# Two running sums for the expert outputs, conditional weight loads, and two weight splits per block on GpSimd, in a decoder layer with 64 experts

## The chip, the cores and the metric

The kernel runs on one core of a Trainium2 chip. The metric is the device time of one execution in microseconds (us), and the smaller the better. The engines are named as in the profile: PE (TensorE, matmul; PEld is its loading of weights), DVE (VectorE), ACT (ScalarE), POOL or Pool (GpSimd), SP (SyncE, which here only issues transfers). Lines such as L1171 are lines of the kernel before, unless the text says that they are of the changed kernel.

## What is computed

One decoder layer on 512 tokens of width 1024, in float32. Three token mixers are projected, gated and summed, and a residual is added. Behind it stands the part that the change touches: a mixture of 64 experts of width 256, eight for each token, and one shared expert, then a residual and a last norm.

```python
def moe_ffn(h, router_w, router_bias, w1, w3, w2, sw1, sw3, sw2):
    scores = sigmoid(xt @ router_w)                 # 512 x 64
    ...                                             # the best 8 of 64 experts for each token, weights W
    for each expert e, for its tokens t:
        out[t] += W[t, e] * ((silu(xt[t] @ w1[e]) * (xt[t] @ w3[e])) @ w2[e])
    out += (silu(xt @ sw1) * (xt @ sw3)) @ sw2      # shared expert
x = x + gate * out
return rmsnorm(x, final_norm)
```

(The loop over experts is written here as what it amounts to.) Which tokens an expert gets is known only on the chip, so the kernel makes lists of work and runs loops whose lengths it reads from them.

## The kernel before

The program is one long order of work. On these inputs it goes through these stages (times of the profiled execution): input projection and the three mixers to 838 us; the gated sum of the projected branches, 838 to 928 us; output projection and routing, 931 to 1060; shared expert and **pairs** of expert runs, 1060 to 1500; **blocks** of what is left, 1508 to 1617; last norm, 1617 to 1644.

Matmuls are done to more than the precision of one pass: each operand is split in a high half (rounded, by ACT, L49) and a low half (the rest, a subtraction, L50), and three matmuls are summed (high by high, low by high, high by low). `split(hi, lo, src)` puts the low half on DVE unless it is told another engine.

An expert's slots fall into runs. A long run (up to 256 slots, "a") and a short one (up to 64, "c") are computed together in `pair_of_runs`; what is left goes by blocks of 128 slots in `block(i)`. There are 16 pairs and 9 blocks here. Both loops are nests of `tc.If(n > i)`, so every engine compares and branches once per turn (L1311, L1316).

One block on the engines:
- PE: the up projection of this block (24 matmuls of 128x512, L1133 to L1135, `ph`), transposes of the next block's tokens (`pt`, L1126), transposes of the activated product (`p`, L1151), the down projection (12 matmuls, `py`, L1163 to L1165).
- ACT and DVE: the splits of the *next* block's weights, six pieces of 128x1024 per block. `wh[u]` on ACT, then `wl[u]` on DVE, for u = 0 to 3 (up, from the raw tile `ra`) and u = 4, 5 (down, from `rad`). Between them stand, in order, the activation `hw` (ACT, then DVE L1143), the splits of the tokens (`mT_hi`, `mT_lo`) and of the activated product (`hh`, `hl`), and `y` (DVE L1167). On DVE the order is wl0, wl1, wl2, hw, wl3, sa, mT_lo, hl, mT_lo, y, y, wl4, wl5.
- Pool: copies the next list row (`ia`, L1102), gathers the tokens (`xg`, L1104), and at the end issues an indirect transfer that adds `y` into the sum `acc` in DRAM (L1171). Each add waits for the one before it on the same sum, since they may hit the same rows.
- SP: loads the raw weights for the block after the next (L990, L996; 3.1 MB per block), into the buffers that the splits have read. It does so also past the end of the list, where the row of the list names some expert anyway.

`acc` is 768 x 1024 floats: 512 tokens and 256 rows for empty slots. It begins as the residual stream, its last 256 rows zeroed by four ACT-queue transfers beside the gated sum (L758). Short runs add to it by halves of rows, through the view `accc` (L1218). At the end four token tiles are loaded from it (`fm`, L1333, issued by SP), squared (ACT L1334), scaled (Pool L1336 and L70, DVE L1338) and stored (L1339).

Of the kernel before, what the change touches and what calls it, by code (L numbers as in the profile page):

```python
# [34 lines left out]
def trunk(ctx, tc, x, c, ada_w, ada_b, norm1, norm2, w_in, conv_a_w, conv_a_b, ln_a_g, ln_a_b,  # L35
# [21 lines left out]
    # ---------------------------------------------------------------- constants  # L57
# [20 lines left out]
    acc = dram.tile([S + 2 * P, D], F32, name="acc")  # L78
# [14 lines left out]
    # ---------------------------------------------------------------- parameters in columns  # L93
# [6 lines left out]
    for name, ap, n in plist:  # L100
        if at % P + n > P or name == "mu":  # the first two are wanted before the others
            at = (at // P + 1) * P
        off[name] = at
        at += n
# [10 lines left out]
    # ---------------------------------------------------------------- input projection  # L115
# [68 lines left out]
    # shift and scale of two channel tiles at a time; the first columns' weights come in between  # L184
# [18 lines left out]
    # RMSNorm statistics and the transposed normalised stream  # L203
# [19 lines left out]
    abv = cols("ab", 16).rearrange("p (z k) -> p z k", z=2)  # of shift and 1 + scale  # L223
# [36 lines left out]
    # ---------------------------------------------------------------- RWKV  # L260
# [17 lines left out]
    zd = dram.tile([16, P, S], F32, name="zd")  # mixed conv 0-3, RWKV 4-7, LRU 8-15  # L278
    gd = dram.tile([24, P, S], F32, name="gd")  # branch gates, tanh of half
# [7 lines left out]
    # masks over (head, s) rows and t columns  # L287
# [4 lines left out]
    mask = rp.tile([P, 2, CH], F32, name="mask")  # s < t, s <= t  # L292
    V.tensor_scalar(mask[:, 0], tcol, srow, None, op0=OP.is_gt)
    V.tensor_scalar(mask[:, 1], tcol, srow, None, op0=OP.is_ge)
    lev = rp.tile([P, 6, CH], BF, name="lev")  # block-doubling masks
# [12 lines left out]
    bones = rp.tile([P, P], F32, name="bones")  # head block of ones  # L308
# [7 lines left out]
    smask = rp.tile([P, S], BF, name="smask")  # 0 where a chunk starts  # L316
# [8 lines left out]
    hcol = rp.tile([P, 12], F32, name="hcol")  # halves of w0, a0, k_a  # L325
# [27 lines left out]
    # ---------------------------------------------------------------- rest of the modulation, as rows  # L353
    def modulation(g4):
# [9 lines left out]
        if g4 // 2 == 2:  # norm2 (1 + scale)  # L364
# [5 lines left out]
    UC = 4           # chunks per unit  # L370
    US = UC * CH     # tokens per unit
    HQ = (slice(0, CH), slice(CH, P))  # rows of either head
    identc = rp.tile([P, CH], F32, name="identc")  # an identity per head
# [6 lines left out]
    def over(t, n=UC):  # the same for each chunk  # L380
        return t[:, None].to_broadcast([t.shape[0], n, *t.shape[1:]])
# [4 lines left out]
    # products per chunk and head: each head has its rows of the array, and its bank  # L386
    class Heads:
# [16 lines left out]
        def turn(s, src):  # L404
            for i in range(UC):
                for h, q in enumerate(HQ):
                    if h:  # a transpose proper leaves its result from row 0 on
# [9 lines left out]
    # a power of a sum over each head's channels, on all of them: token-major for the power, and back  # L417
# [14 lines left out]
    def unit(c, hf):  # L432
# [6 lines left out]
        # sigmoid(x) = (1 + tanh(x / 2)) / 2  # L439
# [5 lines left out]
        # decay: exp(w) = exp(-1/2) sigmoid(w0 + ...), summed within each chunk  # L445
# [7 lines left out]
        # the removal key's norm, squared, goes with the one of its two factors that is summed over  # L453
# [12 lines left out]
        # time-major: rows (head, token). zt: Z, Azk V, V; bt: A_zb^T, A_qb^T, B, K; at: A_zk^T, A_qk^T  # L466
# [16 lines left out]
        # bonus  # L483
# [6 lines left out]
        # T = (I + A)^-1 of 32-token blocks and its transpose, by block doubling  # L490
        inv = rp.tile([P, 2, UC, CH], F32, name="inv", bufs=2)  # T^T, T
# [19 lines left out]
        # [W | U0] = (I + A)^-1 [Z | Azk V], here negated  # L511
# [742 lines left out]
    def block(i):  # L1254
        if i:
            load_up(ra, GL, i + 2)
# [3 lines left out]
        for u in range(4):  # L1260
            up_a(ph, u)
            if u < 3:
                split_a(i + 1, u, up)
# [106 lines left out]
```

## Time and profile before

| | |
|---|---|
| runs, us | 1646.1, 1631.59, 1632.52; median 1632.52 |
| profiled execution: span | 1644.2 us; the run nearest to it is 1646.1 |
| PE busy | 1460.9 us, 89% |
| PEld, DVE | 1045.2 (64%), 1032.0 (63%) |
| ACT, POOL | 611.6 (37%), 580.6 (35%) |

A row of the timeline is start, duration, engine, line, operation, output<-input, then in brackets how long the engine had been idle and what ended that. A row of a table by stretches gives for each engine the busy us in the stretch and the number of instructions, then the TensorE clock that was granted (1.00 is 2.4 GHz, 0.50 is 1.2 GHz), the share of the DMA engines' time and GB/s. Busy shares are means over stages with different limits, so each edit is to be read in the stage where it stands.

### The profile page before, as it was taken

What the parts mean: (1) busy time and instruction counts of PE and PEld (TensorE: products, weight loads), DVE (VectorE), ACT (ScalarE), POOL (GpSimd) and SP (SyncE); (2) the same over time, 40 slices, a digit from 0 to 9 for tenths busy, and PEclk for the clock granted to TensorE, in tenths of its full rate; (3) what the DMA queues carried; (4) which work ended last, traced back from release to release, by engine and by line L of the source; (5) the groups of instructions that cost most, each with busy time, mean ns of one, the idle gap of its engine ahead of it and who ended that gap; (6) DMA issues with size and microseconds to landing.
All of it is one profiled execution on the core that took longest, in us unless ns stands there. A gap on an engine that the chain in (4) does not pass through costs nothing. (4 is left out here: it accounts for less than half of the span.)

```text
span 1644.2 us, 23961 instructions
## 1 busy us (share of the span) xinstructions
PE 1460.9 (89%) x8794; PEld 1045.2 (64%) x8794; DVE 1032.0 (63%) x1803; ACT 611.6 (37%) x981; POOL 580.6 (35%) x457
## 2 busy tenths in 40 slices
PE   4998897989999989999699986797999999997883
PEld 3765565656666666566478764565777777775662
DVE  7747879796843246656825476664656656565884
ACT  4432132222442326336422242152443444433763
POOL 3222433132222223234765266433333334232322
PEclk7989888898999979989899999898999999998997
DMA  9324434021222112113475353499999999996996
GB/s 336 110 76 123 151 90 145 26 81 39 68 85 75 39 30 62 46 39 100 125 245 200 145 169 129 126 321 341 326 330 327 330 324 336 333 327 158 339 312 208
DMA packets 202140, 294.85 MB, mean 179 GB/s; under 512 B 13484, under 2 KB 155062, under 8 KB 202002
## 3 DMA queue, kind: packets, MB, share of 16 engines
q1 hardware_dynamic: 181490, 244.97, 44.3%
q0 software_dynamic: 17904, 44.90, 11.8%
q10 hardware_dynamic: 2608, 3.24, 0.6%
q8 instruction: 74, 1.21, 0.3%
q14 instruction: 64, 0.52, 0.1%
HBM read 258.15 MB, written 45.92 MB: 185 GB/s over the span
## 5 line engine op out<-in xcount | busy, mean ns | idle before, releaser
L50 POOL TENSOR_TENSOR w_lo<-w_raw,w_hi 128x1024 fp32r<-128x1024 f32 x76 | 195.1, 2571 | 335.2 <-ACT w_hi L49 333.2
L53 PE MATMUL ps_in<-hT_hi,w_hi 128*128 128x512 f32 x496 | 216.1, 436 | 5.8 <-ACT hT_hi L49 3.3
L54 PE MATMUL ps_in<-hT_hi,w_lo 128*128 128x512 f32 x496 | 214.2, 432 | 7.2 <-POOL w_lo L50 7.2
L55 PE MATMUL ps_in<-hT_lo,w_hi 128*128 128x512 f32 x496 | 211.6, 430 | 0.0
L50 DVE TENSOR_TENSOR wl<-ra,wh 128x1024 fp32r<-128x1024 f32 x100 | 121.6, 1224 | 105.7 <-ACT wh L49 103.5
L1133 PE MATMUL ph<-wh,mT_hi 128*128 128x512 f32 x360 | 144.9, 403 | 14.0 <-issue 10.1
L49 ACT ACTIVATE wh<-ra 128x1024 fp32r<-128x1024 f32 x100 | 105.9, 1062 | 105.9 <-PE ph L1135 102.4
L1134 PE MATMUL ph<-wl,mT_hi 128*128 128x512 f32 x360 | 143.5, 399 | 0.5 <-DVE wl L50 0.5
L1135 PE MATMUL ph<-wh,mT_lo 128*128 128x512 f32 x360 | 142.8, 397 | 0.0
L1171 POOL DMA_INDIRECT acc<-y,sa x41 | 72.2, 1761 | 155.8 <-DVE hc L1207 121.0
L53 PEld LDWEIGHTS ps_in<-hT_hi,w_hi 128*128 128x128 f32 x496 | 98.1, 198 | 37.7 <-issue 9.6
L54 PEld LDWEIGHTS ps_in<-hT_hi,w_lo 128*128 128x128 f32 x496 | 97.9, 197 | 32.1 <-POOL w_lo L50 8.1
L55 PEld LDWEIGHTS ps_in<-hT_lo,w_hi 128*128 128x128 f32 x496 | 98.2, 198 | 24.5 <-issue 5.0
L597 DVE SCALAR_TENSOR_TENSOR u<-ut,par,u 128x512 f32<-128x512 f32 x120 | 100.1, 857 | 1.2
L49 ACT ACTIVATE w_hi<-w_raw 128x1024 fp32r<-128x1024 f32 x76 | 79.6, 1053 | 56.2 <-PE ps_p L55 27.0
L498 POOL TENSOR_TENSOR Bm<-bt,lev 128x256 f32<-128x256 f32 x40 | 28.8, 736 | 168.3 <-DVE bt L480 101.9
L49 ACT ACTIVATE wh<-rad 128x1024 fp32r<-128x1024 f32 x52 | 52.4, 1055 | 95.4 <-PE py L1165 39.0
L1133 PEld LDWEIGHTS ph<-wh,mT_hi 128*128 128x128 f32 x360 | 69.3, 192 | 29.3 <-issue 11.0
L1167 DVE TENSOR_TENSOR y<-py,rows 128x512 f32<-128x512 f32 x82 | 56.5, 690 | 44.5 <-PE py L1165 43.8
L1134 PEld LDWEIGHTS ph<-wl,mT_hi 128*128 128x128 f32 x360 | 69.3, 193 | 15.2 <-DVE wl L50 1.0
L1135 PEld LDWEIGHTS ph<-wh,mT_lo 128*128 128x128 f32 x360 | 69.2, 192 | 14.5
L1163 PE MATMUL py<-wh,hh 128*128 128x512 f32 x180 | 76.4, 424 | 1.5 <-ACT hh L49 0.7
(524 smaller groups left out, 3105.8 us busy)
## 6 DMA issues: line engine op xcount, KB each, us to landing
ra<-in_exp_w_dram SPq DMA_DIRECT2D x52, 1024.0 KB
rc<-in_exp_w_dram SPq DMA_DIRECT2D x34, 1024.0 KB
w_raw<-in_w_in_dram SPq DMA_DIRECT2D x31, 1024.0 KB
rad<-in_exp_w_dram SPq DMA_DIRECT2D x27, 1024.0 KB
ada<-in_ada_w_dram SPq DMA_DIRECT2D x64, 256.0 KB
rcd<-in_exp_w_dram SPq DMA_DIRECT2D x16, 1024.0 KB
ada<-in_ada_w_dram SPq DMA_DIRECT2D x8, 1024.0 KB
gd<-sg SPq DMA_DIRECT2D x24, 256.0 KB
```

What stands on the lines that cost most here:

```text
L49: A.activation(hi, src, AF.Copy)
L50: (lo_engine or V).tensor_tensor(lo, src, hi.bitcast(F32), op=OP.subtract)
L53: T.matmul(ps, l[0], r[0], start=first, stop=False)
L54: T.matmul(ps, l[1], r[0], start=False, stop=False)
L55: T.matmul(ps, l[0], r[1], start=False, stop=last)
L597: V.scalar_tensor_tensor(u[:, ct], ut[ct][:, w:w + S], col("caw", w * 4 + ct), u[:, ct], op0=OP.mult, op1=OP.add)
L1133: T.matmul(ph[b], h2T[0][b][:, k], wh[u][:, q], start=(k == 0), stop=False)
L1134: T.matmul(ph[b], h2T[0][b][:, k], wl[u][:, q], start=False, stop=False)
L1135: T.matmul(ph[b], h2T[1][b][:, k], wh[u][:, q], start=False, stop=(k == KT - 1))
L1163: T.matmul(py, hT[0][:, k], wh[4 + k][:, q], start=(k == 0), stop=False)
L1167: V.tensor_tensor(y[:, q], py, gate[:, q], op=OP.mult)
L1171: st = G.indirect_dma_start(out=acc, out_offset=IOA(ap=at, axis=0), in_=y, in_offset=None, compute_op=OP.add, bounds_check=S + 2 * P - 1, ...
```

## The change

There are four edits.

1. A second sum `acc2` of the same size. It is zeroed whole by two ACT-queue transfers behind the four that zero the last rows of `acc`. Short runs (through `accc`) add to it; long runs still add to `acc`; blocks add to the two in turn.
2. In `block` the weight loads stand in a `tc.If(n_left > i + 2)`.
3. In `block` the low halves of pieces 0 and 2 are computed by Pool; pieces 1, 3, 4 and 5 stay on DVE.
4. At the end each token tile is loaded from both sums (SP and ACT queue) and DVE adds the two, before the square.

```diff
-    acc = dram.tile([S + 2 * P, D], F32, name="acc")
+    acc, acc2 = (dram.tile([S + 2 * P, D], F32, name=n) for n in ("acc", "acc2"))
...
         nc.scalar.dma_start(acc[S + h // 2 * P:...], z0...)
+    a2v = acc2.rearrange("(g p) d -> p g d", p=P)
+    for h in range(2):
+        nc.scalar.dma_start(a2v[:, :, h * 512:h * 512 + 512],
+                            z0.rearrange("p c x -> p (c x)")[:, None].to_broadcast([P, (S + 2 * P) // P, 512]))
...
-    h2c, accc = (t.rearrange("t (a d) -> (t a) d", a=2) for t in (h2d, acc))
+    h2c, accc = (t.rearrange("t (a d) -> (t a) d", a=2) for t in (h2d, acc2))
...
-    def split_a(j, u, up=None):
-        split(wh[u], wl[u], ...)
+    def split_a(j, u, up=None, lo_engine=None):
+        split(wh[u], wl[u], ..., lo_engine)
...
-    def add_a(y, at, beside=None):
-        st = G.indirect_dma_start(out=acc, ...
+    def add_a(y, at, beside=None, to=acc):
+        st = G.indirect_dma_start(out=to, ...
...
     def block(i):
-        if i:
-            load_up(ra, GL, i + 2)
         up = rc[0] if i == 1 else None
-        load_down(rad[i % 2], GL, i + 2)
+        with tc.If(n_left > i + 2):
+            if i:
+                load_up(ra, GL, i + 2)
+            load_down(rad[i % 2], GL, i + 2)
...
             if u < 3:
-                split_a(i + 1, u, up)
+                split_a(i + 1, u, up, V if u == 1 else G)
...
-        add_a(down_a(hT, gm2), sa[:, 0, 0:1])
+        add_a(down_a(hT, gm2), sa[:, 0, 0:1], to=(acc, acc2)[i % 2])
...
         nc.sync.dma_start(m, acc[t * P:(t + 1) * P])
+        m2 = fp.tile([P, D], F32, name="fm2", bufs=4)
+        nc.scalar.dma_start(m2, acc2[t * P:(t + 1) * P])
+        V.tensor_tensor(m, m, m2, op=OP.add)
         A.activation(sq, m, AF.Square, scale=1.0 / 32, accum_out=fs[:, t:t + 1])
```

How it moves instructions is seen in the order of each engine's program. First Pool, one block, before (L1316 is the loop's branch; `ra`, `wh`, `wl` are raw weights, high and low halves):

```order
L1316 COMPARE_AND_BRANCH
L1101 TENSOR_LOAD items
L1101 ISA x2
L1102 ISA
L1102 COPY ia_8120<-idxw 128x4
L1104 DMA xg_8102<-h2d,ia_8120 128x1024
L1171 DMA acc<-y,sa 768x1024
```

The same block on Pool in the changed kernel (its lines are some numbers higher; wl_7159 and wl_7161 are pieces 0 and 2):

```order
L1323 COMPARE_AND_BRANCH
L1262 COMPARE_AND_BRANCH
L1262 UNCONDITIONAL_BRANCH x2
L50 TENSOR_TENSOR wl_7159<-ra_7921,wh_7153 128x1024
L50 TENSOR_TENSOR wl_7161<-ra_7921,wh_7155 128x1024
L1106 TENSOR_LOAD items
L1106 ISA x2
L1107 ISA
L1107 COPY ia_8123<-idxw 128x4
L1109 DMA xg_8105<-h2d,ia_8123 128x1024
L1177 DMA acc<-y,sa 768x1024
```

Two subtractions and the inner branch now stand ahead of the gather, right behind the add of the block before. On DVE the same block before, up to the low half of the activated product (wl_7156 to wl_7159 are pieces 0 to 3):

```order
L1316 COMPARE_AND_BRANCH
L50 TENSOR_TENSOR wl_7156<-ra_7918,wh_7150 128x1024
L50 TENSOR_TENSOR wl_7157<-ra_7918,wh_7151 128x1024
L50 TENSOR_TENSOR wl_7158<-ra_7918,wh_7152 128x1024
L1143 SCALAR_TENSOR_TENSOR hw<-hw,ia_8120,ph 128x256
L50 TENSOR_TENSOR wl_7159<-ra_7918,wh_7153 128x1024
L1117 COPY sa<-ia_8120 128x4
L50 TENSOR_TENSOR mT_lo_6263<-pt,mT_hi_6261 128x512
L50 TENSOR_TENSOR hl<-p_16619,hh 128x256
```

And on DVE in the changed kernel (wl_7160 and wl_7162 are pieces 1 and 3):

```order
L1323 COMPARE_AND_BRANCH
L1262 COMPARE_AND_BRANCH
L1262 UNCONDITIONAL_BRANCH x2
L50 TENSOR_TENSOR wl_7160<-ra_7921,wh_7154 128x1024
L1149 SCALAR_TENSOR_TENSOR hw<-hw,ia_8123,ph 128x256
L50 TENSOR_TENSOR wl_7162<-ra_7921,wh_7156 128x1024
L1122 COPY sa<-ia_8123 128x4
L50 TENSOR_TENSOR mT_lo_6264<-pt,mT_hi_6262 128x512
L50 TENSOR_TENSOR hl<-p_16625,hh 128x256
```

DVE keeps piece 1 ahead of `hw` and piece 3 behind it; the two pieces that stood around piece 1 are gone. Last, ACT in the tail, before (behind the loop's branches; `fnb` is the last norm's weight row, `fsq` the square):

```order
L1316 UNCONDITIONAL_BRANCH x97
L1329 ACTIVATE fnb<-fnp 128x512
L1334 ACTIVATE fsq,fs<-fm 128x1024
L1329 ACTIVATE fnb<-fnp 128x512
L1334 ACTIVATE fsq,fs<-fm 128x1024 x3
```

And in the changed kernel, where the rows of L1342 are the loads from `acc2` (printed as acc_73) into the four `fm2` tiles:

```order
L1323 UNCONDITIONAL_BRANCH x97
L1342 DMA fm_27765<-acc_73 128x1024
L1342 DMA fm_27776<-acc_73 128x1024
L1336 ACTIVATE fnb<-fnp 128x512
L1342 DMA fm_27787<-acc_73 128x1024
L1336 ACTIVATE fnb<-fnp 128x512
L1344 ACTIVATE fsq,fs<-fm 128x1024 x2
L1342 DMA fm_27798<-acc_73 128x1024
L1344 ACTIVATE fsq,fs<-fm 128x1024 x2
```

The fourth load from `acc2` now stands behind two squares on ACT, which wait for DVE's adds.

## Rows read from the trace of the kernel before

**Rows 1.** The page's head: span of the profiled execution.

```profile
span 1644.2 us, 23961 instructions
```

**Rows 2.** Stretches: busy us per engine, PE clock, DMA share, GB/s.

```profile
core 0: us, PE busy (x) PEld busy (x) DVE busy (x) ACT busy (x) POOL busy (x), PEclk, DMA share, GB/s
852.00:856.00 4.00, 4.00 (x19) 3.23 (x18) 1.72 (x4) 0.83 (x1) 0.00 (x0) 1.00 1.08 384
...
1433.00:1459.00 26.00, 26.00 (x142) 18.96 (x144) 15.66 (x24) 10.99 (x17) 9.45 (x10) 1.00 1.06 333
...
1558.00:1571.00 13.00, 11.36 (x47) 8.60 (x46) 10.04 (x14) 7.96 (x10) 3.30 (x4) 0.87 1.05 332
...
1616.00:1620.00 4.00, 0.55 (x3) 0.11 (x1) 2.96 (x3) 1.94 (x2) 2.32 (x1) 1.00 0.06 14
1628.00:1632.00 4.00, 1.31 (x2) 0.00 (x0) 0.02 (x1) 2.26 (x4) 0.81 (x2) 0.50 0.98 374
```

**Rows 3.** Timeline of one block: start, duration, engine, line, operation, idle before it.

```profile
1544.55 0.39 PE L1133 MATMUL ph<-wh,mT_hi 128*128 128x512 f32 x1
1545.72 2.32 POOL L1171 DMA_INDIRECT acc<-y,sa  x1 [2.49 <-DVE y L1167]
1547.52 1.07 ACT L49 ACTIVATE wh<-ra 128x1024 fp32r<-128x1024 f32 x1 [0.29 <-PE ph L1135]
1547.63 3.58 DVE L50 TENSOR_TENSOR wl<-ra,wh 128x1024 fp32r<-128x1024 f32 x3
...
1550.48 1.05 ACT L49 ACTIVATE wh<-ra 128x1024 fp32r<-128x1024 f32 x1
1551.12 0.47 DVE L1143 SCALAR_TENSOR_TENSOR hw<-hw,ia,ph 128x256 f32<-128x256 f32 x1
...
1551.56 1.23 DVE L50 TENSOR_TENSOR wl<-ra,wh 128x1024 fp32r<-128x1024 f32 x1
...
1553.37 0.41 DVE L50 TENSOR_TENSOR hl<-p,hh 128x256 fp32r<-128x256 f32 x1
...
1553.84 0.51 PE L1165 MATMUL py<-wh,hl 128*128 128x512 f32 x1 [0.49 <-DVE hl L50]
...
1556.25 0.39 PE L1133 MATMUL ph<-wh,mT_hi 128*128 128x512 f32 x1
```

**Rows 4.** Groups by line, 1507 to 1618: count, busy us, mean ns, idle before.

```profile
L1171 POOL DMA_INDIRECT acc<-y,sa x9 | 20.9, 2319 | 24.4 <-DVE y L1167 24.4
```

**Rows 5.** Timeline, output projection: the same subtraction on DVE and Pool.

```profile
932.89 5.78 POOL L50 TENSOR_TENSOR wo_lo<-wr,wo_hi 128x1024 fp32r<-128x1024 f32 x2 [1.14 <-ACT wo_hi L49]
933.78 2.64 DVE L50 TENSOR_TENSOR wo_lo<-wr,wo_hi 128x1024 fp32r<-128x1024 f32 x1 [0.67 <-ACT wo_hi L49]
```

**Rows 6.** Line L50, two of its groups: ns of one, min/median/max.

```profile
L50 DVE TENSOR_TENSOR wo_lo<-wr,wo_hi x4: 1224/1675/2642, 931.9 to 946.9; 128x1024 fp32r<-128x1024 f32 x4
L50 POOL TENSOR_TENSOR wo_lo<-wr,wo_hi x4: 2452/2929/3369, 932.9 to 948.0; 128x1024 fp32r<-128x1024 f32 x4
```

**Rows 7.** Timeline, gated sum, behind the zeroing: weights landing, split, used.

```profile
855.17 2.01 ACT L49 ACTIVATE w_hi<-w_raw 128x1024 fp32r<-128x1024 f32 x2 [3.42 <-DMA w_raw<-in_proj_b_dram]
856.31 4.91 POOL L50 TENSOR_TENSOR w_lo<-w_raw,w_hi 128x1024 fp32r<-128x1024 f32 x2 [8.59 <-ACT w_hi L49]
...
860.82 0.40 PE L54 MATMUL ps_p<-z_hi,w_lo 128*128 128x512 f32 x1
```

**Rows 8.** Timeline of the tail: first and last square, last scaling.

```profile
1629.74 1.06 ACT L1334 ACTIVATE fsq<-fm 128x1024 f32<-128x1024 f32 x1 [2.56 <-DMA fm<-acc]
...
1634.06 1.06 ACT L1334 ACTIVATE fsq<-fm 128x1024 f32<-128x1024 f32 x1
...
1638.13 1.28 DVE L1338 SCALAR_TENSOR_TENSOR fm<-fm,fs,fnb 128x1024 f32<-128x1024 f32 x1 [0.77 <-POOL fs L70]
```

**Rows 9.** Line L1316, PE's branches at the turns of the block loop, ns.

```profile
L1316 PEldq COMPARE_BRANCH  x11: 65/65/3336, 1507.4 to 1617.6; - x11
```

**Rows 10.** Timeline, pairs: the Pool adds that wait for the add before.

```profile
1122.20 1.59 POOL L1171 DMA_INDIRECT acc<-y,sa  x1 [5.65 <-DMA acc<-yc,sc__8497]
...
1482.43 2.06 POOL L1218 DMA_INDIRECT acc<-yc,sc__12172  x1 [7.72 <-DMA acc<-y,sa]
...
1505.96 1.59 POOL L1218 DMA_INDIRECT acc<-yc,sc__12434  x1 [5.60 <-DMA acc<-y,sa]
```

More of the change, by code (lines that the diff above doesn't have):

```diff
@@ L1118, in slots @@
         return t
-    def split_a(j, u, up=None):
-        split(wh[u], wl[u], (up or ra[j % 2])[:, u * 1024:(u + 1) * 1024] if u < 4 else rad[j % 2][:, (u - 4) * 1024:(u - 3) * 1024])
+    def split_a(j, u, up=None, lo_engine=None):
+        split(wh[u], wl[u], (up or ra[j % 2])[:, u * 1024:(u + 1) * 1024] if u < 4 else rad[j % 2][:, (u - 4) * 1024:(u - 3) * 1024],
+              lo_engine)
     def x_a(b, g):
@@ L1168, in down_a @@
         return y
-    def add_a(y, at, beside=None):
-        st = G.indirect_dma_start(out=acc, out_offset=IOA(ap=at, axis=0), in_=y, in_offset=None,
+    def add_a(y, at, beside=None, to=acc):
+        st = G.indirect_dma_start(out=to, out_offset=IOA(ap=at, axis=0), in_=y, in_offset=None,
                                   compute_op=OP.add, bounds_check=S + 2 * P - 1, oob_is_err=True)
```

## The prediction

> **What bounds the kernel now.** I read the page's head first, then the table by stretches, because the change touches four stages with different limits. The span is 1644.2 us [rows 1]; the run nearest to it is 1646.1, so 1.9 us lie around the span and the profiled execution's own time is 1646.1, 0.8% above the median of 1632.52. In the pairs PE is busy 26.00 us of 26 [rows 2]: PE bounds them, and only what makes PE wait there can cost or gain anything. In the gated sum PE is also full while the DMA engines are full too (4.00 of 4, share 1.08, 384 GB/s at 852 to 856) [rows 2], so a transfer added there stands in line with those that PE needs. In the tail PE has nothing to do; the transfers (374 GB/s) [rows 2], the squares and the scalings are the path.
>
> In a block PE is the bound, but not alone. The timeline of one block shows it: PE starts at 1544.55 and the next block at 1556.25, 11.70 us later, and before the down projection's first use of `hl` PE had to wait for DVE (1553.84, idle 0.49, ended by `hl`) [rows 3]. Behind that stands a chain on DVE: wl0 to wl2 end at 1551.21, `hw` at 1551.59, wl3 at 1552.79, then `sa`, `mT_lo` and `hl`, which ends at 1553.78 [rows 3]. wl3 begins when ACT's wh3 is done (1551.53) [rows 3]. So whatever delays wl3 delays `hl` and with it PE, one for one; nothing lies between to take it up.
>
> **The sum of two parts, by turns (edit 1).** In the blocks each add should wait for the add before it. The groups by line show that it never did: all nine adds of the block stage had their idle time, 24.4 us in all, ended by DVE's `y`, none by an add [rows 4]. Gain there: 0. In the pairs three adds did wait for another sum's landing: 5.65, 7.72 and 5.60 us, 19.0 in all [rows 10]. These waits vanish, but Pool is not what ends the stage: PE is full through the pairs [rows 2]. I take 0; if that cover did not hold, up to 19.0 would be gained (a rival below). The waits' removal also lets Pool leave the pairs earlier, so the halves that it now makes for the first block start without delay; that is why I add nothing for that one.
>
> **Zeroing `acc2`.** 768 x 1024 x 4 bytes are 3.15 MB. At the 384 GB/s of a full stretch [rows 2] that is 8.2 us of all DMA engines, in a stage where they are full. What is late next is the raw weights of the gated sum: they landed at 855.17, Pool's first low half from them began at 856.31 and two of them took 4.91, so the first was ready near 858.8, and PE used one first at 860.82 at the latest [rows 7]. Slack 2.0. If the zeros go ahead of those weights whole, PE stalls 8.2 - 2.0 = 6.2; if the weights' queue keeps its turn, nothing. I take the middle, **3** (0 to 6).
>
> **Weight loads behind a condition (edit 2).** Two blocks of nine no longer load, 2 x 3.1 MB. The DMA engines were at a share of 0.06 at 1616 to 1620 and nothing in the block's path waits for them [rows 2, 3]; gain 0. The inner condition costs each engine a compare and a jump per block. PE's compare takes 65 ns in the median [rows 9]; 9 x 2 x 65 ns is 1.2 at most, run ahead by the sequencer while matmuls drain. I take 0 (0 to 1.2).
>
> **Two low halves on Pool (edit 3).** DVE loses two subtractions of 1.2 us per block. What that could gain: `hw` began at 1551.12 though ACT's part of it was done when ACT began wh3 at 1550.48, so up to 0.6 on `hw`; but wl3 still waits for wh3, which ended 0.03 before wl3 began [rows 3], so the path to `hl` gains about nothing. What it could cost: Pool takes 2.45 for what DVE does in 1.22 [rows 6], and the two do not run side by side. Where both did this same subtraction, DVE's began at 933.78, during Pool's (932.89 to 935.34), and ended at 936.42: 1.08 behind Pool's end, 2.64 instead of 1.22; the Pool operation behind it took 3.3 (5.78 for the two; 3.37 at most) [rows 5, 6]. I lay that pattern into the block, in us from the block's start:
>
> - Pool is free when its add is issued: it begins at 1.17 and takes 2.32 [rows 3], or 1.59 as adds do in the pairs [rows 10]: free at 2.76 to 3.49. wl0 ends at 5.2 to 5.9.
> - DVE's wl1 is ready at 4.04 (wh1 ends at 1548.59) [rows 3], in the middle of wl0: held, it ends at 6.3 to 7.0. `hw` ends at 6.8 to 7.5; before, 7.04.
> - Pool's wl2 begins at 5.2 to 5.9, shares time with wl1, takes 3.37: ends at 8.6 to 9.3.
> - DVE's wl3 is ready at 7.0 to 7.5: held by wl2, it ends 1.08 after it, at 9.65 to 10.4; before, 8.24 [rows 3].
>
> So `hl`, the down projection and the next block come 1.4 to 2.15 later in each of nine blocks [rows 4]: 12.7 to 19.4, I take **16**. The `hw`, `mT_lo` and `hl` operations read PSUM; I count no hold for them. The Trainium skill, page "SBUF — State Buffer", section "Who interferes with whom", speaks against this edit: a DVE instruction with two SBUF inputs contends with a GpSimd instruction that reads SBUF, and the second to issue fully blocks. The trace agrees that DVE is held to beyond the end of Pool's operation; by the rule the held one would end a whole 1.22 after it rather than 1.08, which would make this term 1.3 larger.
>
> **The clock.** PE's idle time before the down projection grows from about 0.5 to between 1.9 and 2.6 per block. One block before the change already lost time to the clock: in 1558 to 1571 the granted clock was 0.87 of full, that is 13 x 0.13 = 1.7 us [rows 2]. Longer gaps should bring it in more blocks. I count four more of nine, **7** (0, none; 15, all).
>
> **The tail (edit 4).** Twice as much is loaded: 0.52 MB per load at 374 GB/s [rows 2] is 1.4 us. Tile 0 is complete one load later than its first square began, 1629.74 + 1.4 = 1631.1; tile 1 is complete 2.8 later, at 1633.9; DVE adds (1.2, [rows 6]) and ACT squares (1.06): 1636.2. Only then does ACT issue the last load from `acc2`; ACT idled 2.56 for the first load [rows 8], so it lands at 1638.8 or later, is added by 1640.0, and the last square begins 6 later than the 1634.06 of before [rows 8]. From there the end is the same work (last scaling at 1638.13). I take **6** (4, if Pool's small steps are shorter when less crowded; 8).
>
> **The sum.** 3 + 0 + 16 + 7 + 6 = 32. On the profiled execution that is 1646.1 + 32 = 1678; on the median of the runs, 1632.5 + 32 = **1664**. With all low bounds 16.7 (1649), with all high ones 48.4 (1681).
>
> **The rivals.**
>
> *The hold costs nothing here* (0.24): Pool's operations fall where DVE waits anyway, or DVE gets through. For it: DVE is idle part of each block; against it: the ready times above fall inside Pool's operations by 1 us and more. Then only zeroing and tail are left: 1632.5 + 3 + 6 = 1641.5, between 1636 and 1647, since freeing DVE gives next to nothing.
>
> *The waits on the sum were on the path* (0.12), the case on the other side. The adds stand in Pool's order ahead of the gathers, and a late gather is late tokens for PE. If all 19.0 us [rows 10] reached PE, with 1.7 each of lost clock [rows 2], 24 are gained and 9 paid for zeroing and tail, and the hold costs nothing: 1632.5 - 24 + 9 = 1617.5 (1608 to 1623). It is faster than before from the point where more than 9 of the 19 lie on the path. Against it: 26.00 of 26 in the pairs, and the last wait, at 1505.96, lies where all engines leave the loop.
>
> *The inner jump is dear* (0.10). Of PE's eleven branches at L1316 the longest took 3336 ns, the way out of the loop [rows 9]. If the jump over the other arm of the inner condition costs as much in each of nine blocks, 9 x 3.3 = 30 are added: 1694. Against it: ten of eleven fell within about 65 ns, though those went straight on. The Trainium skill, page "Runtime: NRT & Kernel Launch", section "Instruction fetch mechanics", says that a taken branch whose target is outside the fetched window forces a fetch; here the other arm is short, and no row of before shows a short jump.
>
> **How the numbers follow.** My forecast, 1664 (1649 to 1681), has 0.54. A measurement of this kernel can tell about 1% (16.3 us: 1616.2 and 1648.8) from no change. Slower by over 1%: nearly all of the forecast and the dear jump, 0.61. Within 1%: the hold that costs nothing and the weaker part of the waits on the path, 0.32. Faster: its stronger part, 0.07. The range that leaves out no more than 2 in 10 takes in the forecast and the first rival, from 1635 to 1683.
>
> **What would show it.** In the profile after: DVE's wl1 and wl3 in the blocks should take well over 1.22 (wl1 2.0 to 3.0, wl3 2.2 to 3.4), Pool's two halves 5.8 together, blocks should begin every 13.1 to 13.9 us, and PE's idle time before L1171 of the changed kernel (the first use of `hl`) should be ended by DVE and be 1.9 us or more; more stretches of the block stage should show a granted clock under 0.9. If blocks still begin every 11.7, the hold is wrong. The gated sum should be up to 6 longer, with PE waiting near 861 for a low half. The last square should begin about 10 after the first. If the pairs end earlier than before in relation to their start, the waits on the sum were on the path. If PE's compares at the inner condition show microseconds, the jump is dear.

## The result and the profile after

The changed kernel takes 1686.28 us (median of 4 runs, 1681.33 to 1687.5); the kernel before, timed beside it, 1634.19 (4 runs). The ratio is 1.0301, 95% interval 1.0253 to 1.0349: some 41 to 57 us slower. 32 had been forecast. It is slower, as forecast, but it lies 3 us above the upper end of the range (1683).

The profiled execution of the changed kernel took 1681.33, its span is 1679.5. Where did the time go? The same four stages are laid side by side in the table by stretches, here with their true ends in either trace (gated sum; pairs from the first transpose of a short run's tokens to the last down matmul; blocks from the first up matmul to the last down matmul; tail). First before:

```profile
core 0: us, PE busy (x) PEld busy (x) DVE busy (x) ACT busy (x) POOL busy (x), PEclk, DMA share, GB/s
838.00:927.50 89.50, 89.43 (x383) 72.06 (x384) 43.39 (x53) 19.63 (x29) 39.68 (x18) 1.00 0.52 182
1068.34:1496.94 428.60, 415.67 (x2208) 302.39 (x2208) 253.85 (x357) 177.60 (x249) 147.84 (x129) 0.98 1.04 324
1507.66:1616.15 108.49, 93.78 (x414) 71.81 (x414) 90.13 (x114) 70.42 (x89) 29.94 (x26) 0.97 0.95 288
1616.15:1644.20 28.05, 4.51 (x6) 0.99 (x4) 8.10 (x7) 7.35 (x12) 8.32 (x9) 0.58 0.50 171
```

Then the changed kernel:

```profile
832.00:930.40 98.40, 92.70 (x384) 74.00 (x384) 40.92 (x53) 19.40 (x29) 38.91 (x19) 0.97 0.56 198
1066.03:1494.65 428.62, 415.00 (x2207) 301.80 (x2208) 253.18 (x357) 178.04 (x249) 154.47 (x129) 0.98 1.04 324
1505.68:1643.15 137.47, 105.33 (x413) 82.93 (x414) 103.23 (x96) 70.16 (x89) 74.31 (x44) 0.84 0.64 181
1643.15:1679.50 36.35, 4.50 (x6) 0.99 (x4) 12.73 (x11) 7.60 (x12) 7.38 (x9) 0.57 0.55 190
```

The gated sum is 8.9 longer, the blocks 29.0, the tail 8.3: 46 together. The pairs take 428.60 before and 428.62 after. The rest of the program, which the change leaves alone, was 11 shorter in this execution: 6.0 of it in the part ahead of the gated sum, which takes 827 to 839 us in the traces of this case, whatever was changed. So this is put down to chance; the runs of either kernel differ by 6 to 15. By the medians the change costs 52, not 46. The other 6 lie in no trace that was kept: the profiled execution was the fastest of its four, with a mean granted clock of 0.918 where the other three had 0.909 to 0.912.

The number of PE's operations in the blocks is the same, so the second number of a row splits the 29.0: PE's idle time went from 108.49 - 93.78 = 14.7 to 137.47 - 105.33 = 32.1, that is +17.4, and its busy time from 93.8 to 105.3, +11.6, because the granted clock fell from 0.97 to 0.84 in the mean. (This says what PE did, not yet what each cause cost: the run that keeps PE busy, below, splits the 29.0 otherwise.)

What PE waited for is in the timeline of one block (the block that begins at 1597.83):

```profile
1599.01 2.31 POOL L1177 DMA_INDIRECT acc<-y,sa  x1 [3.86 <-DVE y L1173]
...
1601.93 5.21 DVE L50 TENSOR_TENSOR wl<-ra,wh 128x1024 fp32r<-128x1024 f32 x1 [0.94 <-ACT wh L49]
...
1607.06 0.47 DVE L1149 SCALAR_TENSOR_TENSOR hw<-hw,ia,ph 128x256 f32<-128x256 f32 x1
1607.45 1.21 DVE L50 TENSOR_TENSOR wl<-ra,wh 128x1024 fp32r<-128x1024 f32 x1
1607.58 0.69 PE L1157 MATMUL p<-ident,hw 128*128 128x128 f32 x2 [3.67 <-DVE hw L1149]
```

Pool's two halves in the same block, by Pool's own rows:

```profile
1600.79 2.96 POOL L50 TENSOR_TENSOR wl<-ra,wh 128x1024 fp32r<-128x1024 f32 x1
...
1603.36 2.68 POOL L50 TENSOR_TENSOR wl<-ra,wh 128x1024 fp32r<-128x1024 f32 x1
```

The second ends at 1606.04. DVE's piece 1, ready at 1601.93, ends at 1607.14: 1.1 behind *both*, 5.21 instead of 1.22. `hw`, next on DVE, is held up with it, and PE idles 3.67 before `p`. In the block of [rows 3] it was 1.06:

```profile
1551.66 0.44 PE L1151 MATMUL p<-ident,hw 128*128 128x128 f32 x2 [1.06 <-DVE hw L1143]
```

Piece 3 comes when Pool is done and takes 1.21; `hl` is in time. So the hold is there, on another operation and in another shape than forecast. Seven of nine blocks look like this. The first two don't; in the first:

```profile
1509.82 2.41 POOL L50 TENSOR_TENSOR wl<-ra,wh 128x1024 fp32r<-128x1024 f32 x1 [9.84 <-ACT wh L49]
1511.19 2.11 DVE L50 TENSOR_TENSOR wl<-ra,wh 128x1024 fp32r<-128x1024 f32 x1 [14.15 <-ACT wh L49]
1512.61 2.93 POOL L50 TENSOR_TENSOR wl<-ra,wh 128x1024 fp32r<-128x1024 f32 x1 [0.38 <-ACT wh L49]
...
1514.14 2.49 DVE L50 TENSOR_TENSOR wl<-ra,wh 128x1024 fp32r<-128x1024 f32 x1 [0.40 <-ACT wh L49]
```

There DVE gets in between the two (1513.30, 1.1 behind the first) and piece 3 is held by the second: the pattern of [rows 5], as the forecast had laid it into all nine.

In the gated sum the rows that answer to [rows 7]:

```profile
857.32 1.06 ACT L49 ACTIVATE w_hi<-w_raw 128x1024 fp32r<-128x1024 f32 x1 [11.54 <-DMA w_raw<-in_proj_b_dram]
...
858.42 0.49 PE L53 MATMUL ps_p<-z_hi,w_hi 128*128 128x512 f32 x1 [3.65 <-ACT w_hi L49]
858.45 4.69 POOL L50 TENSOR_TENSOR w_lo<-w_raw,w_hi 128x1024 fp32r<-128x1024 f32 x2 [17.12 <-ACT w_hi L49]
...
860.86 0.79 PE L54 MATMUL ps_p<-z_hi,w_lo 128*128 128x512 f32 x1 [1.94 <-POOL w_lo L50]
861.46 0.63 PE L55 MATMUL ps_p<-z_lo,w_hi 128*128 128x512 f32 x1
```

The raw weights landed 25.2 us into the stage, before 17.1: 8.1 later, about all of the 8.2 that the zeros take. The zeros did not go ahead of them, though: from 838 to 854 the queue of the zeros (q10) and that of the loads (q1) moved bytes side by side, and by 854 nearly all of the zeros were through.

```profile
q10 hardware_dynamic: 1849, 3.65, 58.9%
q1 hardware_dynamic: 1779, 2.82, 46.5%
```

(Packets, MB, share of the 16 DMA engines; from 844 to 856 in the kernel before it is 0.87 MB on q10 and 3.82 on q1.) PE waited 3.65 and 1.94 for them, and the matmuls behind take 0.63 instead of 0.40: the granted clock was 0.50 from 860 for 6.8 us. In the tail, rows that answer to [rows 8]:

```profile
1658.56 1.23 DVE L1343 TENSOR_TENSOR fm<-fm,fm 128x1024 f32<-128x1024 f32 x1 [12.03 <-DMA fm<-acc]
...
1663.07 0.33 ACTq L1342 DMA_DIRECT2D fm<-acc  x1
...
1668.81 1.28 DVE L1348 SCALAR_TENSOR_TENSOR fm<-fm,fs,fnb 128x1024 f32<-128x1024 f32 x1 [0.77 <-POOL fs L70]
1670.02 1.22 DVE L1343 TENSOR_TENSOR fm<-fm,fm 128x1024 f32<-128x1024 f32 x1
1671.27 1.06 ACT L1344 ACTIVATE fsq<-fm 128x1024 f32<-128x1024 f32 x1 [4.43 <-DVE fm L1343]
```

The fourth load from the second sum is issued behind the second square, at 1663.07; its addition begins only at 1670.02, right behind the third scaling (1668.81 to 1670.09), after which it stands in DVE's order.

### The profile page after: what moved, and what is told of

It is laid out like the page before. It is cut to its first block, busy times and chain, and to the rows that moved or that the text cites. A ratio compares the mean times of both kernels' runs of the same rounds, so it can differ in the third digit from the quotient of the medians.

```text
span 1679.5 us, 24063 instructions
## 1 busy us (share of the span) xinstructions
PE 1468.4 (87%) x8794; PEld 1052.9 (63%) x8794; DVE 1048.5 (62%) x1789; ACT 611.6 (36%) x981; POOL 630.9 (38%) x475
## 3 DMA queue, kind: packets, MB, share of 16 engines
q0 software_dynamic: 17904, 44.90, 11.7%
q8 instruction: 74, 1.21, 0.3%
## 5 line engine op out<-in xcount | busy, mean ns | idle before, releaser
L50 POOL TENSOR_TENSOR w_lo<-w_raw,w_hi 128x1024 fp32r<-128x1024 f32 x76 | 195.3, 2574 | 344.9 <-ACT w_hi L49 342.9
L50 DVE TENSOR_TENSOR wl<-ra,wh 128x1024 fp32r<-128x1024 f32 x84 | 132.8, 1584 | 113.8 <-ACT wh L49 107.2
L53 PEld LDWEIGHTS ps_in<-hT_hi,w_hi 128*128 128x128 f32 x496 | 98.3, 198 | 38.9 <-issue 10.7
L1169 PE MATMUL py<-wh,hh 128*128 128x512 f32 x180 | 80.8, 449 | 1.0 <-ACT hh L49 0.9
L1171 PE MATMUL py<-wh,hl 128*128 128x512 f32 x180 | 76.9, 428 | 4.3 <-DVE hl L50 4.3
```

The source lines that it names most:

```text
L50: (lo_engine or V).tensor_tensor(lo, src, hi.bitcast(F32), op=OP.subtract)
L53: T.matmul(ps, l[0], r[0], start=first, stop=False)
L1169: T.matmul(py, hT[0][:, k], wh[4 + k][:, q], start=(k == 0), stop=False)
L1171: T.matmul(py, hT[1][:, k], wh[4 + k][:, q], start=False, stop=(k == 1))
```

## The experiments

They ran later, on two chips (3 and 5), on which the kernel before takes 1627.5 to 1628.6 in the median; ratios are to that. Where a kernel ran once, its time stands in place of a ratio. "Stage" is the block stage, 108.5 in the trace of before, unless another is named. Theory A says that the loss is a sum of separate terms (halves with their clock, zeroing, tail), B that the half clock has another cause than the halves, C that the inner condition or the alternating sums are what costs.

| run | ratio (interval) | block stage, us |
|---|---|---|
| changed kernel (the result above) | 1.0301 (1.0253 to 1.0349) | 137.5 |
| halves back on DVE | 1.0118 (1.0073 to 1.0162) | 108.3 |
| halves alone | 1.0245 (1.0206 to 1.0284) | 140.6 |
| zeroing early | 1.0268 (1.0229 to 1.0306) | 139.0 |
| condition alone | 0.9998 (0.9967 to 1.0029) | 109.8 |
| two sums, made cheap | 1.0043 (1.0020 to 1.0066) | 112.4 |
| halves, PE kept busy | 1.0130 (1.0084 to 1.0175) | 134.2 |
| halves, Pool begins later | 1661.5 us, one run | 141.4 |
| halves, after a pause | 1667.4 us, one run | 152.9 |
| Pool writes only | 1631.3 us, one run | 110.2 |
| Pool reads two | 1668.6 us, one run | 153.1 |
| pieces 2 and 3 later | 0.9979 (0.9955 to 1.0003) | 104.7 |
| piece 3 alone on Pool | 0.9963 (0.9941 to 0.9985) | 106.6 |

**The halves, taken out and alone.** The first run undoes edit 3 in the changed kernel, the second does it alone in the kernel before.

```diff
-                split_a(i + 1, u, up, V if u == 1 else G)
+                split_a(i + 1, u, up)
```

> The changed kernel with all six low halves of a block on DVE again; two sums, condition and tail as changed. Theory A (four separate terms; in the two traces the blocks cost 29.0 us more, of it 17.4 PE idle time and 11.5 matmuls at half clock; the gated sum 8.7, the tail 8.3): blocks of 11.7 us again, ratio to the kernel before 1.010, about 1651. Theory B (the halves cost only PE's idle time, the half clock comes from somewhere else, for instance the inner branch): blocks of about 13, about 1663. Theory C (the inner condition and the alternating sums are the main cost): about 1680.

```diff
-                split_a(i + 1, u, up)
+                split_a(i + 1, u, up, V if u == 1 else G)
```

> The kernel before with the two low halves per block on Pool and nothing else. Theory A: the block stage takes 29 us more (108.9 to 138), about 1663. Theory B: 17 more, about 1651. Theory C: under 5 more, about 1638. In A the DVE operation between the two Pool operations takes 5.2 us in most blocks, also without the inner branch.

Without the halves the stage is 108.3, with PE's clock at 0.97 as before; with nothing but the halves it is 140.6 at 0.82:

```profile
1488.12:1596.45 108.33, 93.79 (x414) 71.78 (x414) 90.14 (x114) 70.34 (x89) 29.94 (x26) 0.97 0.77 229
```

```profile
1485.48:1626.10 140.62, 107.74 (x413) 84.71 (x414) 104.38 (x96) 70.35 (x89) 75.63 (x45) 0.82 0.77 223
```

(First fence: halves back on DVE; second: halves alone.) All of the blocks' loss, wait and clock, comes and goes with edit 3, and without the inner condition too: B falls. The two runs are 1.2% and 2.4% over the kernel before, 3.6% together, against 3.0% for the whole change; their intervals allow that.

**The condition alone** (edit 2 in the kernel before).

```diff
-            load_up(ra, GL, i + 2)
+        with tc.If(n_left > i + 2):
+            if i:
+                load_up(ra, GL, i + 2)
...
```

> The kernel before with the condition on the weight loads and nothing else. Theory A: the branches are run ahead, nothing changes, 1634 (within 3). Theory C: each of nine inner branches costs 1 to 3 us, 1643 to 1660. Last blocks without loads gaining time: under 1634 by more than 5.

0.9998: neither gain nor loss. The alternating sums don't cost either: with the halves back on DVE they were still in, and the stage took 108.3. C falls. In the trace of the changed kernel PE's compares at the inner condition took 169 ns in the median, 223 at most, none of them microseconds:

```profile
L1262 PEldq COMPARE_BRANCH  x16: 65/169/223, 1505.2 to 1624.8; - x16
```

**The zeros moved.** The changed kernel, with the second sum zeroed from the SP queue in the recurrent mixer's stage.

```diff
+    zc = lp.tile([P, 256], F32, name="zc")
+    G.memset(zc, 0.0)
...
+    for h in range(4):
+        nc.sync.dma_start(a2v[:, :, h * 256:h * 256 + 256], zc[:, None].to_broadcast([P, (S + 2 * P) // P, 256]))
...
-    for h in range(2):
-        nc.scalar.dma_start(a2v[:, :, h * 512:h * 512 + 512], ...)
```

> The changed kernel with the second sum zeroed some 200 us earlier, by the SP queue in the recurrent mixer's stage, where the DMA engines moved under 80 GB/s. Theory A: the 8.7 us of the gated sum go (PE's wait for a low half at 858 and the 6.8 us at half clock behind it), about 1677 where the changed kernel has 1686. Rival: the gated sum was long by chance or for another reason, no change.

The zeros were issued at 464 to 474 us, some 360 ahead of the gated sum and not the 200 of the expectation. The gated sum takes 89.47 again (98.3 in the changed kernel), with a clock of 1.00:

```profile
829.00:918.30 89.30, 89.30 (x384) 71.95 (x383) 44.00 (x53) 19.33 (x28) 38.95 (x18) 1.00 0.53 183
```

1.0268 against 1.0301 is 5 us by the medians, where the intervals overlap; the stage itself shows all of it. The zeros were the cause, and where they stand now no cost shows: the gated sum begins at 828.8 us here, at 832.1 in the changed kernel.

**Two sums, made cheap.** The halves on DVE, the zeros early, and the tail written in order: eight loads first, each addition ahead of the scalings that can wait.

```diff
+        for t in range(TT):
...
+            nc.sync.dma_start(m, acc[t * P:(t + 1) * P])
+            nc.scalar.dma_start(m2, acc2[t * P:(t + 1) * P])
...
+        add(0)
+        add(1)
+        for t in range(2, TT):
+            add(t)
+            scale(t - 2)
...
```

> The changed kernel with all halves on DVE, the second sum zeroed early as in the run above, and the tail written out in order: all eight loads issued first, each addition ahead of the scalings. Theory A: blocks and gated sum as in the kernel before, only the tail's double load is left, tail of 31 to 33 us instead of 28, ratio 1.002 to 1.004. Rival (the two sums do gain something that the costs hid): under 1.000.

1.0043, still slower than before. The tail is 34.4, less than the 36.4 of the changed kernel, more than the 31 to 33 that were expected; the block stage was 3.9 longer in this execution, with two more stretches at half clock. Nothing that the costs hid comes to light: two sums gain nothing here.

**PE kept busy in the gap.** The halves alone, and twelve matmuls into a tile that nobody reads where PE waits for `hw`.

```diff
+        idle = psx.tile([P, 512], F32, name="phc")
+        for k in range(12):
+            T.matmul(idle, wl[5][:, :P], wh[4][:, :512], start=True, stop=True)
         hT = turn_a([hw])[0]
```

> The run with the halves alone on Pool, and in each block twelve more matmuls of 128x512 (2.8 us at full clock) into a PSUM tile that nobody reads, put where PE waits for hw; what is computed for the output is the same. If the half clock is a cost of its own, brought by PE's 4 us of idle time: the clock stays at 1.00 in the blocks, and the block stage goes from 138 to 141 us back to about 126 to 129, so about 1 per cent over the kernel before instead of 2.4. Rival (the half clock comes whatever PE does, or the extra matmuls lengthen the path): 141 or more.

```profile
1486.54:1620.69 134.15, 120.09 (x522) 92.64 (x522) 104.15 (x96) 70.42 (x89) 75.70 (x45) 0.96 0.80 235
```

The clock stays up (0.96 instead of 0.82), so it is PE's idle time that brings it down. But the stage falls by 6.5, not by the 12 to 15 expected: 134.2. One block in which the clock was at 1.00 throughout:

```profile
1563.44 0.39 PE L1134 MATMUL ph<-wh,mT_hi 128*128 128x512 f32 x1
...
1573.27 0.44 PE L1152 MATMUL p<-ident,hw 128*128 128x128 f32 x2 [1.01 <-DVE hw L1144]
...
1575.40 0.50 PE L1166 MATMUL py<-wh,hl 128*128 128x512 f32 x1 [0.44 <-DVE hl L50]
...
1577.81 0.39 PE L1134 MATMUL ph<-wh,mT_hi 128*128 128x512 f32 x1
```

It takes 14.37, 2.67 more than the 11.70 of [rows 3], with no slow matmul in it: so much costs the hold by itself. With the halves alone matmuls took 14.0 longer (107.74 against 93.78), and only some 6.5 of that was on the path: at half clock PE no longer waits for `hl` in the held blocks, at full clock it waits 0.44 for it again.

**When does DVE get in between?** In the trace of the changed kernel Pool's first half began inside DVE's last subtraction in the seven bad blocks. This run moves it behind that by a Pool write of zeros.

```diff
+        G.memset(xc[:, :256], 0.0)
         for u in range(4):
```

> The halves alone on Pool, with a write of 128x256 zeros by Pool ahead of the first half in each block, so that it no longer begins inside DVE's last subtraction of the block before. In the traces the DVE operation between the halves took 2.1 to 3.2 us where Pool's first half did not begin inside a DVE subtraction (two blocks of nine), 5.2 where it did (seven). If that overlap is what lets Pool's second half go first: DVE's piece 1 takes 2 to 2.6 and piece 3 2.5 to 3 in all nine blocks, PE idles 3.3 per block instead of 3.7. Rival (the first two blocks differ for another reason, such as their place behind the pairs): still 5.2 in seven.

The expectation failed: Pool's first half now begins 0.05 behind DVE's subtraction, and piece 1 still takes 5.2 to 5.5 in eight of nine blocks. What remains different between good and bad blocks is how Pool's own operations follow one another. In the bad ones the first half is recorded to begin 0.4 to 0.6 before Pool's add (or write of zeros) ends, and the second half 0.4 to 0.6 before the first ends; in the good ones the second begins after the first, or at most 0.05 before its end. The next run lets Pool wait for piece 1's high half first, so that it has paused.

```diff
...
+                if u == 1:
+                    G.tensor_copy(xc[:, :2], wh[1][:, :2].bitcast(F32))
+                    G.tensor_tensor(wl[0], (up or ra[(i + 1) % 2])[:, :1024], wh[0].bitcast(F32), op=OP.subtract)
```

> The halves alone on Pool, but Pool first waits for piece 1's high half (4.0 us into the block), so that it has been idle when its first half begins. DVE's piece 1 then begins first and takes 1.2. If DVE gets in between two Pool operations unless Pool's first began on the heels of the add's issue: piece 3 on DVE, begun inside Pool's first half, takes about 2, and Pool's two do not overlap in the records by more than 0.1; blocks of about 12.3. Rival (two Pool operations in a row always go ahead of DVE here): piece 3 takes 3.5 or more, blocks of 14 or more.

```profile
1557.51 2.36 POOL L1270 TENSOR_TENSOR wl<-ra,wh 128x1024 fp32r<-128x1024 f32 x1
...
1559.22 1.75 DVE L50 TENSOR_TENSOR wl<-ra,wh 128x1024 fp32r<-128x1024 f32 x1 [0.40 <-ACT wh L49]
1559.85 3.31 POOL L50 TENSOR_TENSOR wl<-ra,wh 128x1024 fp32r<-128x1024 f32 x1
1560.89 2.30 DVE L1117 COPY sa<-ia 128x4 int32<-128x4 int32 x1
...
1564.16 0.79 PE L1166 MATMUL py<-wh,hl 128*128 128x512 f32 x1 [3.43 <-DVE hl L50]
```

DVE's subtraction, begun in Pool's first, gets in between (1.75, ends 1.1 behind the first), and Pool's second waits for it (3.31): as expected, in all nine blocks. The blocks got no shorter for it, 17.0 instead of the 12.3 expected, because the next operation on DVE, a copy of 128x4 integers that takes 0.16 elsewhere, was held 2.30 by Pool's second half, and `hl` behind it. That copy had been counted at nothing. In all these kernels the overlap of Pool's second operation with its first goes along with who went first; whether it decides that or only follows from it, no run here shows.

**Is it Pool's reading?** Two runs on the kernel before, in which nothing waits for what Pool makes.

```diff
+        for _ in range(2):
+            G.memset(xg[1], 0.0)
```

> The kernel before (all low halves on DVE), and at the start of each block Pool writes 128x1024 zeros twice into a tile that the blocks don't use: Pool busy as long as with the halves, but without reading. If Pool's reading holds DVE: DVE's subtractions stay at 1.22, blocks at 11.7, the block stage at 109. Rival (any long Pool operation holds DVE, or Pool's lateness at its gather and add costs): subtractions over 2, the block stage over 125.

```diff
+        for _ in range(2):
+            G.tensor_tensor(xg[1], gm2, gm2, op=OP.subtract)
```

> The kernel before (all low halves on DVE), and at the start of each block Pool subtracts two 128x1024 inputs in SBUF twice into a tile that the blocks don't use; DVE does all its work as before and nothing waits for Pool's results. If the hold by Pool's reads is the cause, not the late halves themselves: a DVE subtraction of the block takes 3.5 to 5.5, PE idles 3 or more before p and the block stage takes 138 or more. Rival (what costs is that the two halves come late): 109.

Writing only, then reading two inputs, at the same place in a block:

```profile
1556.02 2.54 POOL L1261 MEMSET xg<- 128x1024 f32 x2
1556.15 3.58 DVE L50 TENSOR_TENSOR wl<-ra,wh 128x1024 fp32r<-128x1024 f32 x3
```

```profile
1554.18 2.31 POOL L1171 DMA_INDIRECT acc<-y,sa  x1 [3.80 <-DVE y L1167]
1555.96 5.30 POOL L1261 TENSOR_TENSOR xg<-rows 128x1024 f32<-128x1024 f32 x2
1556.08 7.40 DVE L50 TENSOR_TENSOR wl<-ra,wh 128x1024 fp32r<-128x1024 f32 x3
```

Beside Pool's writes DVE's three subtractions take 1.19 each as ever (the writes took 2.54, half of what was meant); beside Pool's subtractions, whose results nobody uses, they take 7.40, and the stage is 153.1. So it is not that two halves came late: Pool's subtractions slow DVE's by being there, and its writes of zeros don't.

This run also narrows the question before it. Pool's first subtraction begins 0.5 before its add ends (1556.49), as in the bad blocks, and still DVE gets in between the two in all nine blocks; the second begins 0.08 behind the first's end (1558.42):

```profile
1558.50 2.77 POOL L1261 TENSOR_TENSOR xg<-rows 128x1024 f32<-128x1024 f32 x1
```

So an early begin of the first operation is not enough for Pool to go twice.

**DVE's order, and a piece where DVE doesn't mind.** What could a version gain that respects this? First without Pool: pieces 2 and 3 behind the splits that PE waits for.

```diff
-            if u < 3:
+            if u < 2:
                 split_a(i + 1, u, up)
...
-        split_a(i + 1, 3, up)
...
         x_a(0, 1)
+        split_a(i + 1, 2, up)
+        split_a(i + 1, 3, up)
```

> The kernel before with the splits of pieces 2 and 3 of a block moved behind the splits of the tokens and of the activated product, on ACT and DVE; one sum, nothing on Pool. If DVE's order is what PE waits for (1.64 us per block), hw comes 0.5 earlier and hl is no longer waited for: blocks of 10.8 to 11.2 instead of 11.7, 5 to 8 us less in all, ratio 0.995 to 0.997. Rival (DVE with 10.9 us of work per block becomes the bound, or the delayed y and pieces 4 and 5 make PE wait at the next block): no change or slower.

Blocks of 11.1 instead of 11.7, as expected, but one took 15.7 and the ratio, 0.9979 (0.9955 to 1.0003), is not clear of no change. In that block two transfers were late: the raw weights, whose buffer is now freed later, and the add before. So here, in this one block of nine, an add did wait for the one before:

```profile
1540.27 1.59 POOL L1171 DMA_INDIRECT acc<-y,sa  x1 [5.56 <-DMA acc<-y,sa]
1541.31 1.06 ACT L49 ACTIVATE wh<-ra 128x1024 fp32r<-128x1024 f32 x1 [3.93 <-DMA ra<-in_exp_w_dram]
```

Then piece 3 alone on Pool, which comes when DVE has only operations with an input in PSUM (and the small copy just ahead of it).

```diff
-        split_a(i + 1, 3, up)
+        split_a(i + 1, 3, up, G)
```

> The kernel before with one low half per block on Pool, piece 3, whose turn comes when DVE has only operations with an input in PSUM until y. If the hold concerns only DVE operations with both inputs in SBUF: nothing on DVE is held, hl no longer queues behind piece 3, PE's idle time falls from 1.64 to about 1.1 per block, 4 to 5 us less in all, ratio 0.997. Rival (Pool's later gather makes PE wait for tokens, or hl and mT_lo are held too): 1.000 or more.

```profile
1528.85 0.16 DVE L1117 COPY sa<-ia 128x4 int32<-128x4 int32 x1
1528.95 2.39 POOL L50 TENSOR_TENSOR wl<-ra,wh 128x1024 fp32r<-128x1024 f32 x1 [3.56 <-ACT wh L49]
...
1529.38 0.69 DVE L50 TENSOR_TENSOR mT_lo<-pt,mT_hi 128x512 fp32r<-128x512 f32 x1 [0.37 <-ACT mT_hi L49]
...
1529.99 0.41 DVE L50 TENSOR_TENSOR hl<-p,hh 128x256 fp32r<-128x256 f32 x1
```

0.9963 (0.9941 to 0.9985): some 6 us faster than the kernel before, and so faster than the changed one, with one line changed and one argument added. Inside Pool's 2.39 DVE's `mT_lo` and `hl`, with one input in PSUM, take their usual 0.69 and 0.41. Four blocks in a row take 11.0, and PE's idle time in them falls from 1.64 to 1.1. One block of nine took 15.4: the raw weights were late, at a DMA share of 1.07 and 335 GB/s over the blocks ahead of it, and with `hw` late the small copy came behind Pool's begin and was held 1.94. That points to the transfers as the next bound; no run tests it.

## Why the prediction was right or wrong

**What bounds a block** was right: DVE's order is PE's path, and what is put into it delays PE one for one.

**The hold** (16, low and high 12.7 and 19.4) is the first step that failed, in its working and in its size. Its lines on wl1 ("held, it ends at 6.3 to 7.0") and wl2 ("shares time with wl1") took from [rows 5] that DVE gets in between Pool's two operations. In seven of nine blocks it did not: wl1 ended at 9.3 in the block shown, `hw` at 9.7 instead of 6.8 to 7.5, and the wait stood before `p`, not before `hl`. `p` came 2.6 later than before (9.75 us into the block against 7.11), where the forecast had `hl` 1.4 to 2.15 later. PE's idle time grew by 17.4, close to the 16, but that is luck: the idle time leaves out what the slow clock hides. With the clock up such a block costs 2.67, so seven cost 19. In the first two, which follow the forecast's pattern, PE's first use of `hl` came 0.9 and 2.1 later (12.0 us into the block against 11.1, and 11.4 against 9.3). Together that is some 22, an estimate from these rows, above the upper bound. The Trainium skill, page "SBUF — State Buffer", section "Who interferes with whom", was weighed in the forecast; its rule that the second to issue fully blocks is borne out for one Pool subtraction against one of DVE, with 1.1 us from Pool's end to DVE's, not 1.22. In the seven blocks Pool's second half went ahead of a DVE subtraction that was recorded to begin 1.4 earlier (1601.93 against 1603.36), which that rule would not give. The same section says that a GpSimd instruction that only writes SBUF does not contend; the run with Pool's writes agrees (1.19 each).

**The clock** (7, four more blocks of nine) came out in size, not in its working. In all nine blocks, not in four more, an idle time of 2.9 to 3.7 us was followed by a granted clock of 0.50 for 3.4 to 6.8 us, and PE's busy time grew by 11.6. But the 29.0 of the blocks less 22 for the hold leave some 7 for it on the path, and keeping PE busy gave back 6.5. That nine smaller losses add up to the four that were counted is luck as well.

**Zeroing** (3, range 0 to 6) measured 8.9. The slack, the weights that are late next and PE's place of waiting were right. What failed is the alternative that the middle was taken of, "if the weights' queue keeps its turn, nothing": the two queues did move side by side, and the weights, which landed when the zeros were through, came 8.1 later all the same. The range also left out the clock that PE's wait takes along: 5.7 idle, 3.3 longer busy.

**The tail** (6, at most 8) measured 8.3. That the last load is issued behind the second square was right. That it is in use some 2.6 behind its issue was not: it was 6.95, because its addition stands behind the third scaling in DVE's order, which the forecast left out of the chain. The last square began 10.2 later in the stage (28.1 us into it against 17.9) where 6 had been forecast; 1.9 of that came back behind it. With the tail written in order, and all loads issued first, it took 34.4 instead of 36.4.

**The terms at nothing** were right: pairs 428.60 and 428.62, with these waits gone, so their 19.0 us [rows 10] were not on the path; the condition 0.9998. With that the two rivals "waits on the sum" and "inner jump" fall, and "the hold costs nothing" falls with the run of the halves alone.

So the sum of 32 should have been 46, by the same four terms: 3 for 8.9, 16 for some 22, 7 for some 7, 6 for 8.3. The hold was too small because DVE was held over two Pool operations and not one, the zeroing because sharing was taken to cost nothing and PE's wait was priced without the slow matmuls that follow it, the tail because an instruction ahead in DVE's order was left out.

## What to carry to other kernels

Moving work from a busy DVE to an idle Pool paid here only where DVE, meanwhile, had no operation that reads two inputs from SBUF (or a small copy) in the way of something that is waited for; one piece at such a place was worth 0.4%, two pieces at another place cost 2.5%. Price a new wait of TensorE together with the slow matmuls behind it (in the gated sum 3.3 us of them behind a wait of 5.7), but not by adding PE's idle and busy time: part of the slow matmuls fills waits that would come anyway. Price a transfer that is issued into a full stretch with its whole length. Before splitting a sum in two, look whether any add waited for another, and whether that wait was on the path.

## What the runs showed of the hardware that was not expected

- A DVE subtraction with both inputs in SBUF was held over two Pool subtractions in a row (4.9 to 5.5 us) in all blocks in which Pool's second is recorded to begin 0.4 to 0.6 before its first ends; where the second begins at most 0.06 before, or after, the DVE operation went ahead of it (1.6 to 3.4, the shorter the later it began in Pool's first) and Pool's second was the one that waited (2.8 to 3.4). Held, it ended 1.1 behind Pool's end each time.
- A DVE copy of 128x4 integers was held 1.94 to 2.33 by a Pool subtraction; alone it takes 0.16.
- With PE's idle time at 1.64 per block, in two pieces, the clock stood at 1.00 in seven of nine blocks of the kernel before; in the changed kernel, with 2.9 to 3.7 per block, it went to 0.50 in every block, and twelve matmuls that nobody needs, put into the gap, kept it at 1.00 in seven of nine.
- Two DMA queues that were full at once moved bytes side by side (3.65 and 2.82 MB in 16 us), and loads that land last still came later by nearly the whole 8.2 us of the other queue's transfer.
